# A hybrid decoder layer on one core: x transposed by the host, the surplus loop behind the last block, the last norm's sums on other engines

## The chip, the core and the metric

The kernel runs on one core of a Trainium2 chip. A core has TensorE (PE in the profile, its weight loads PEld), VectorE (DVE), ScalarE (ACT), GpSimd (POOL) and SyncE (SP), which here only issues transfers. Each engine works through its own list in order. The metric is the device time of one execution in microseconds; less is better. 0.2% of it is 2.7 us.

## The reference

One layer over 1024 positions of width 1024. The parts that this change touches are the head, the mixer's input, and the end:

```python
mod = silu(c) @ W_ada + b_ada            # shift/scale/gate of both sub-layers
h = x * (1 + scale1) + shift1
proj = h @ w_in                          # 3592 columns: DeltaNet q,k,v,z, beta, decay; attention q,k,v
mix = concat(gated_delta(proj), dilated_attention(proj)) @ w_o
x = layer_norm(ALPHA * x + (1 + gate1) * mix, ln1_g, ln1_b)
h = x * (1 + scale2) + shift2
y = sum over the top 2 of 8 experts of the best of 4 groups: gate * ((silu(h Wg) * (h Wu)) Wd)
x = layer_norm(ALPHA * x + (1 + gate2) * y, ln2_g, ln2_b)
```

## The kernel before

**Head.** x is kept with its 1024 features on the partitions, as eight column pieces (k) of 128 features in two halves (hf) of 512 positions. SP loads `x_` as eight row tiles of 512 KB, four of them ahead of the first 1024 columns x 2 of the modulation weights (`wad`, eight tiles of 1 MB, seven buffers) and four behind them. `x_cols` transposes each half on PE (L209) and copies it out of PSUM (L211, VectorE and ScalarE in turn). PE makes the shift and scale rows from `wad` (`pmod`), a transpose brings them to columns (`modc`, `s1`). Then, for each piece, ScalarE writes the rounded h (`hhi`, L247), VectorE the same in full precision (`ht`, L249), and their difference `hlo` (L251) is taken by VectorE for even k and by GpSimd for odd k.

**Projections.** 28 tasks of 128 columns each follow. A weight tile `wraw` is split into `whi` (ScalarE, L257) and `wlo` (GpSimd, L260), and 48 matmuls of 128x512 make one task: `hhi*whi`, `hlo*whi` and `hhi*wlo` for each piece. The weights of the first task are loaded between the seventh and the eighth `wad`. DeltaNet, attention, the output projection, the first norm and the router follow.

**Experts.** The slots are 81 blocks of 32 rows in the fixed order `SEQ`. A block's work is `block_gu` (64 matmul records `ph`), `block_h` (`pt`, `hT`), `block_d` (32 records `po`, scaled to `yo` on VectorE L1395) and a scatter of `yo` into `y2d` by GpSimd (L1346). In the loop the down projection of block n-1 stands between the up projection and the transpose of block n. Each expert's weights come as 4 MB (`wgu`, L1005) and 2 MB (`wd`, L1010) through SP into rings; after the last of them SP loads `xall`, the 4 MB of the residual (L1503), into a ring slot. Names such as `wgu<-x1d` or `wgu<-y2d` are such ring slots with other contents.

**Surplus loop.** Rows that found no place in the fixed blocks are handled in `overflow`, a loop whose trip count `nov` is read on the device. Every engine loads `novi` (L1398), compares and branches (L1450), and a barrier over all five engines that waits for the outstanding transfers stands at it. In the profiled execution its body is not run: the trace has 81 blocks. The call stands before the last block, after `down(n - 1)`.

**Last norm.** SP loads the norm's rows `lnb` (L1507), then the eight 1 MB pieces of `y2d` (L1531), one for each 128 positions t with the two expert outputs of a position, `ya` and `yb`. `combine(t)` adds them, on GpSimd for t in `PADD` (2, 5) and with PE and an identity into PSUM for the other six, adds the residual and sums (L1546, VectorE), and squares on ScalarE (L1549). `norm(t)` takes the inverse root on GpSimd (L465), applies the mean and the gain (L1556, VectorE) and the factor and offset: for t in `PSCALE` (1, 3, 5, 6) ScalarE L1558 and GpSimd L1559, for the others VectorE L1561. SP stores the result (L1562).

The order on each engine comes from the scheduler of the framework that builds the kernel; SP's and ACT's transfers share eight completion semaphores in turn, so a transfer waits for the one eight places ahead.

Of the kernel before, what the change touches and what calls it, by code (L numbers as in the profile page):

```python
# [20 lines left out]
P = 128  # L21
D = 1024
# [101 lines left out]
def build(nc, tc, I, out):  # L124
# [7 lines left out]
    with es:  # L132
# [25 lines left out]
        w_in = I["w_in"][0].rearrange("(k p) n -> p k n", p=P)  # L158
        wp = hps.enter_context(tc.tile_pool(name="wp", bufs=2, side="right"))

        def load_raw(col):
            raw = wp.tile([P, KD, P], F32, name="wraw", bufs=WR)
            SY.dma_start(raw, w_in[:, :, col:col + P])
            return raw
# [16 lines left out]
        xt = []  # L181

        def load_x(t):
            x_ = ap_.tile([P, D], F32, name="x_", bufs=NT)
            SY.dma_start(x_, I["x"][0, t * P:(t + 1) * P, :])
            xt.append(x_)
# [16 lines left out]
        hst, hlo = {}, {}  # L203

        def x_cols(hf, pool, tag):
            for k in range(KD):
                px = pool.tile([P, 4, P], F32, name=tag, bufs=3)
                for t in range(4):
                    T.transpose(px[:, t, :], xt[hf * 4 + t][:, k * P:(k + 1) * P], ident)  # L209
                hst[k, hf] = hp.tile([P, 512], F32, name="hlo", bufs=2 * KD + 1)  # L210
                (A.copy if k % 2 else V.tensor_copy)(hst[k, hf], px.rearrange("p a b -> p (a b)"))  # L211

        x_cols(0, pa, "px")
# [24 lines left out]
        V.tensor_scalar(s1, mcol[:, 8:16], 1.0, None, op0=OP.add)  # L238
        for hf in range(2):
            if hf == 1:  # L240
                pas.close()
                pps = ExitStack()
                pp = pps.enter_context(tc.tile_pool(name="pp", bufs=2, space=PSUM))
                x_cols(1, pp, "pg")
            for k in range(KD):
                sl_ = slice(hf * 512, hf * 512 + 512)
                A.activation(hhi[:, k, sl_], hst[k, hf], AF.Identity, bias=mcol[:, k:k + 1], scale=s1[:, k:k + 1])  # L247
# [138 lines left out]
        SY.dma_start(w8, w_in[:, :, 4 * GW:4 * GW + 8])  # L386
# [1103 lines left out]
        for n, (i, b_) in enumerate(blocks):  # L1490
# [17 lines left out]
            if n == nb - 1:  # L1508
                down(n - 1)
                overflow()  # L1510
# [16 lines left out]
        PSCALE = (1, 3, 5, 6)  # L1527
        PADD = (2, 5)
# [4 lines left out]
        def combine(t):  # L1533
            ya, yb = (yall[t // 4][:, t % 4, k] for k in range(2))
            if t in PADD:
                G.tensor_tensor(ya, ya, yb, op=OP.add)
                ps = ya
            else:
                ps = pf_.tile([P, D], F32, name="ps", bufs=4)
                for hf in range(2):  # L1540
                    for k, y_ in enumerate((ya, yb)):
                        mm(ps[:, 512 * hf:512 * hf + 512], ident, y_[:, 512 * hf:512 * hf + 512], start=(k == 0),
                           stop=(k == 1))
            xa = xall[:, t]
            mv = fp.tile([P, 8], F32, name="mv", bufs=4)
            V.tensor_tensor_reduce(xa, ps, xa, 1.0, 0.0, OP.add, OP.add, mv[:, 0:1])  # L1546
# [5 lines left out]
        def norm(t, mv):  # L1552
# [51 lines left out]
```

## Time and profile before

| | |
|---|---|
| time, median of 3 runs | 1374.77 us (1373.95 to 1376.49) |
| profiled execution | 1380.62 us, span 1378.8 us |
| busy in the span | PE 1206.5, PEld 823.5, DVE 622.7, POOL 435.3, ACT 334.0 us |
| mean granted TensorE clock | 0.941 |
| HBM read / written | 286.56 MB / 26.89 MB |

The span runs from the first to the last instruction; the profiled execution's own time has 1.8 us around it, and the median of the runs is 5.9 us below it. A row of the timeline gives start, busy time, engine, line, operation, output and inputs, count, and in brackets the idle time before it with what ended it. [...] Times in rows are microseconds from the start of the span.

### The profile page before, as it was taken

To read this page: it belongs to the slowest core of one execution; us is meant where nothing else is said; L and a number is where in the kernel's file an instruction comes from. 1 tells how busy PE (TensorE), PEld (TensorE's weight loads), DVE (VectorE), ACT (ScalarE), POOL (GpSimd) and SP (SyncE) were. 2 spreads that over 40 slices of the span, in tenths; PEclk is the share of its full clock that TensorE was granted. 3 is DMA by queue.
4 is the path that set the end of the run, shared out by engine and by line. 5 is a ranking of instruction groups with operands and counts; after the bars stand their busy time and mean duration, and the time that the engine had idled before them with its cause. 6 is when DMAs were issued, how large, how long until landed. Compare 5 with 4: busy or idle time off the path is not lost.

```text
span 1378.8 us, 32445 instructions
## 1 busy us (share of the span) xinstructions
PE 1206.5 (88%) x13949; PEld 823.5 (60%) x13949; DVE 622.7 (45%) x1414; ACT 334.0 (24%) x753; POOL 435.3 (32%) x410
## 2 busy tenths in 40 slices
PE   5889999999998989989889359898899999999662
PEld 2577787878785767867667235554455555555320
DVE  0867476583726747577986721111111111111126
ACT  1454343433322433344211101010011111111003
POOL 0613223322323404131542433332233333332116
PEclk8899999999999989999998679999999999999976
DMA  9311011110113435343336859999999999999763
GB/s 363 92 31 46 18 47 33 31 43 22 48 48 123 133 119 161 119 182 98 134 134 244 369 218 421 423 422 423 424 417 419 378 421 423 425 421 428 328 248 151
DMA packets 77189, 311.13 MB, mean 226 GB/s; under 512 B 11186, under 2 KB 47780, under 8 KB 67828
## 3 DMA queue, kind: packets, MB, share of 16 engines
q1 hardware_dynamic: 62624, 282.60, 52.3%
q0 software_dynamic: 8928, 21.00, 4.0%
q10 hardware_dynamic: 5492, 5.44, 1.2%
q8 instruction: 111, 1.82, 0.5%
q14 instruction: 34, 0.28, 0.1%
HBM read 286.56 MB, written 26.89 MB: 227 GB/s over the span
## 4 chain that ended last, share of the span: by engine, by line
PE 38%; DMA 13%; DVE 10%; issue 4%; POOL 4%; ACT 1%; POOLq 0%; ACTq 0%; SPq 0%; DVEq 0%
PE ph L128 16%; PE po L128 8%; DMA wd<-in_k_wd 8%; PE pj L128 5%; DMA araw<-in_w_ada 2%; DMA wgu<-x1d 2%; PE pc L128 2%; PE pg L128 2%; PE pt L1382 1%; DVE acc L276 1%; PE px L1362 1%; POOL wlo L260 1%; DVE oh L1037 1%; POOL mv L465 1%; PE pg L804 1%
## 5 line engine op out<-in xcount | busy, mean ns | idle before, releaser
L128 PE MATMUL ph<-wgu,xT 128*32 128x256 f32 x5184 | 300.1, 384 | 8.8 <-DMA wgu<-x1d 8.8
L128 PEld LDWEIGHTS ph<-wgu,xT 128*32 128x32 f32 x5184 | 160.7, 111 | 123.4 <-issue 26.8
L128 PE MATMUL pj<-hhi,whi 128*128 128x512 f32 x448 | 195.2, 436 | 4.4 <-ACT akq L517 2.4
L128 PE MATMUL pj<-hlo,whi 128*128 128x512 f32 x448 | 182.0, 406 | 3.4 <-DVE hlo L251 2.9
L128 PE MATMUL pj<-hhi,wlo 128*128 128x512 f32 x448 | 181.9, 406 | 0.0
L128 PE MATMUL po<-wd,hT 128*32 128x256 f32 x2592 | 157.5, 384 | 20.5 <-DMA wd<-in_k_wd 18.9
L260 POOL TENSOR_TENSOR wlo<-wraw,whi 128x256 fp32r<-128x256 f32 x112 | 95.7, 884 | 233.1 <-ACT whi L257 210.0
L1340 POOL DMA_INDIRECT xg<-h2d,idxt x81 | 82.6, 1020 | 273.4 <-PE px L1362 266.1
L1377 DVE TENSOR_TENSOR th<-th,ph 128x128 f32<-128x128 f32 x81 | 23.4, 288 | 312.7 <-ACT th L1376 312.7
L128 PEld LDWEIGHTS po<-wd,hT 128*32 128x32 f32 x2592 | 85.2, 111 | 78.3 <-issue 22.8
L1346 POOL DMA_INDIRECT y2d<-yo,sct x81 | 82.0, 1013 | 77.1 <-DVE hT L1384 36.0
L128 PEld LDWEIGHTS pj<-hhi,whi 128*128 128x128 f32 x448 | 86.2, 192 | 21.5 <-ACT akq L517 2.8
L128 PEld LDWEIGHTS pj<-hlo,whi 128*128 128x128 f32 x448 | 86.5, 193 | 19.6 <-DVE hlo L251 4.8
L128 PEld LDWEIGHTS pj<-hhi,wlo 128*128 128x128 f32 x448 | 85.8, 191 | 17.6 <-issue 0.5
L1395 DVE SCALAR_TENSOR_TENSOR yo<-po,gat,g2t 128x256 f32<-128x256 f32 x81 | 39.2, 484 | 116.7 <-PE po L128 116.7
L1376 ACT ACTIVATE th<-ph 128x128 f32<-128x128 f32 x81 | 22.5, 278 | 273.6 <-PE ph L128 273.6
L1364 ACT COPY xT<-px 128x256 f32<-128x256 f32 x81 | 30.2, 373 | 205.8 <-PE px L1362 205.8
L128 PE MATMUL pg<-akq 128*128 128x512 f32 (+3 forms) x96 | 40.6, 538 | 9.1 <-DVE sm L789 6.4
L128 PE MATMUL pj<-wohi,mhi 128*128 128x512 f32 x112 | 46.7, 417 | 0.0
L128 PE MATMUL pj<-wo,mhi 128*128 128x512 f32 x112 | 46.3, 413 | 0.0
L128 PE MATMUL pj<-wohi,mlo 128*128 128x512 f32 x112 | 45.3, 405 | 0.0
L128 PE MATMUL pc<-vtk,PT 128*128 128x128 f32 x288 | 39.5, 282 | 5.4 <-ACT PT L806 5.0
(718 smaller groups left out, 1838.2 us busy)
## 6 DMA issues: line engine op xcount, KB each, us to landing
wgu<-in_k_wgu SPq DMA_DIRECT2D x32, 4096.0 KB, 25.6
wd<-in_k_wd SPq DMA_DIRECT2D x32, 2048.0 KB
araw<-in_w_ada SPq DMA_DIRECT2D x32, 512.0 KB, 4.0
wraw<-in_w_in SPq DMA_DIRECT2D x28, 512.0 KB, 4.1
wad<-in_w_ada SPq DMA_DIRECT2D x8, 1024.0 KB, 9.6
wgu<-y2d SPq DMA_DIRECT2D x8, 1024.0 KB, 17.0
xr<-in_x SPq DMA_DIRECT2D x8, 512.0 KB
x1d<-xh POOLq DMA_DIRECT2D x8, 512.0 KB, 2.9
```

The lines of the kernel that those rows point to most:

```text
L128: return T.matmul(o, l, r, start=start, stop=stop)
L260: G.tensor_tensor(lo[:, k:k + 2], raw[:, k:k + 2], hi[:, k:k + 2].bitcast(F32), op=OP.subtract)
L276: V.scalar_tensor_tensor(state["acc"], raw, sc[:, k:k + 1], state["acc"], op0=OP.mult, op1=OP.add)
L465: G.tensor_tensor(o, x, e.to_broadcast(list(x.shape)), op=OP.pow)
L804: T.transpose(p[:, b_ - b0, :], sc_[:, b_ * P:(b_ + 1) * P], ident)
L1037: V.tensor_scalar(o_, e_, f_, None, op0=OP.is_equal)
L1340: G.indirect_dma_start(out=xg, out_offset=None, in_=h2v, in_offset=bass.IndirectOffsetOnAxis(ap=idx, axis=0), bounds_check=4 * S - 1, oob_ ...
L1346: G.indirect_dma_start(out=y2v[b_], out_offset=bass.IndirectOffsetOnAxis(ap=idx, axis=0), in_=yo, in_offset=None, bounds_check=8 * S - 1, ...
L1364: A.copy(xT, px)
L1376: A.activation(th, ph[:, 0], AF.Silu)
L1377: V.tensor_tensor(th, th, ph[:, 1], op=OP.mult)
L1395: V.scalar_tensor_tensor(yo, po, gcol, g2t, op0=OP.mult, op1=OP.mult)
```

## The change

The host hands over x already transposed (`k_xt`, partition = feature within a piece, then half, piece, position), the projection weights regrouped so that a task's tile is one run of 4 KB on each partition (`k_win`), and the eight small columns likewise (`k_w8`). The loads of x, `x_cols`, its 64 transposes and its 16 copies go. SP loads the first task's weights, then all eight `wad` (eight buffers), then x in four pieces of 1 MB. For odd k the full-precision h is now made by ScalarE, and all sixteen differences are taken by VectorE.

```diff
-        for t in range(4):
-            load_x(t)
+        first_w = load_raw(GW)
         wad = []
         for k in range(KD):
-            w = ap_.tile([P, 2048], F32, name="wad", bufs=KD - 1)
+            w = ap_.tile([P, 2048], F32, name="wad", bufs=KD)
             SY.dma_start(w, I["w_ada"][0, k * P:(k + 1) * P, 0:2048])
             wad.append(w)
-            if k == KD - 2:
-                first_w = load_raw(GW)
-        for t in range(4, NT):
-            load_x(t)
+        xT = ap_.tile([P, 2, KD, 512], F32, name="xT", bufs=1)
+        for hf in range(2):
+            for k in range(0, KD, 4):
+                SY.dma_start(xT[:, hf, k:k + 4], I["k_xt"][:, hf, k:k + 4])
...
-                ht = ap_.tile([P, 512], F32, name="ht", bufs=3)
-                V.tensor_scalar(ht, hst[k, hf], s1[:, k:k + 1], mcol[:, k:k + 1], op0=OP.mult, op1=OP.add)
-                hlo[k, hf] = hp.tile([P, 512], F32R, name="hlo", bufs=2 * KD + 1)
-                (G if k % 2 else V).tensor_tensor(hlo[k, hf], ht, hhi[:, k, sl_].bitcast(F32), op=OP.subtract)
+                x_ = xT[:, hf, k]
+                A.activation(hhi[:, k, sl_], x_, AF.Identity, bias=mcol[:, k:k + 1], scale=s1[:, k:k + 1])
+                ht = ap_.tile([P, 512], F32, name="ht", bufs=2)
+                if k % 2:
+                    A.activation(ht, x_, AF.Identity, bias=mcol[:, k:k + 1], scale=s1[:, k:k + 1])
+                else:
+                    V.tensor_scalar(ht, x_, s1[:, k:k + 1], mcol[:, k:k + 1], op0=OP.mult, op1=OP.add)
+                hlo[k, hf] = hp.tile([P, 512], F32R, name="hlo", bufs=2 * KD)
+                V.tensor_tensor(hlo[k, hf], ht, hhi[:, k, sl_].bitcast(F32), op=OP.subtract)
```

The surplus loop is called after the last block:

```diff
-            if n == nb - 1:
-                down(n - 1)
-                overflow()
             gx(n + XB - 1)
             th = block_gu(xp_, pm_, xTs.pop(n), wts[i][0])
...
-            if 0 < n < nb - 1:
+            if n:
                 down(n - 1)
...
         down(nb - 1)
+        overflow()
```

In the last norm VectorE adds the two expert outputs for t in `DADD`; PE adds them for the other six, and for t in `ASUM` also the residual, which ScalarE then copies out of PSUM while it sums. The factor and offset are VectorE's for all eight t.

```diff
-        PSCALE = (1, 3, 5, 6)
-        PADD = (2, 5)
+        DADD, ASUM = (0, 4), (1, 3, 5, 7)
...
-            if t in PADD:
-                G.tensor_tensor(ya, ya, yb, op=OP.add)
+            xa = xall[:, t]
+            if t in DADD:
+                V.tensor_tensor(ya, ya, yb, op=OP.add)
...
-                    for k, y_ in enumerate((ya, yb)):
+                    ys = (xa, ya, yb) if t in ASUM else (ya, yb)
+                    for k, y_ in enumerate(ys):
...
-            V.tensor_tensor_reduce(xa, ps, xa, 1.0, 0.0, OP.add, OP.add, mv[:, 0:1])
+            if t in ASUM:
+                A.activation(xa, ps, AF.Identity, accum_out=mv[:, 0:1])
+            else:
+                V.tensor_tensor_reduce(xa, ps, xa, 1.0, 0.0, OP.add, OP.add, mv[:, 0:1])
...
-            if t in PSCALE:
-                A.mul(xa, xa, mv[:, 4:5])
-                G.tensor_tensor(xa, xa, lnb[:, 1], op=OP.add)
-            else:
-                V.scalar_tensor_tensor(xa, xa, mv[:, 4:5], lnb[:, 1], op0=OP.mult, op1=OP.add)
+            V.scalar_tensor_tensor(xa, xa, mv[:, 4:5], lnb[:, 1], op0=OP.mult, op1=OP.add)
```

Three places show how the lists move; between them every engine's list is the same as before. First, SP's list at the program's start, before (`kc` holds the constants, `wraw` projection weights, `wad` modulation weights):

```order
L137 DMA kc<-in_k_main 128x896
L185 DMA x__90<-in_x 128x1024
L185 DMA x__92<-in_x 128x1024
L185 DMA x__94<-in_x 128x1024
L185 DMA x__96<-in_x 128x1024
L193 DMA wad<-in_w_ada 128x2048 x7
L163 DMA wraw<-in_w_in 128x8x128
L193 DMA wad<-in_w_ada 128x2048
L185 DMA x__116<-in_x 128x1024
```

and in the changed kernel:

```order
L137 DMA kc<-in_k_main 128x896
L162 DMA wraw<-in_k_win 128x1024
L184 DMA wad<-in_w_ada 128x2048 x8
L189 DMA xT<-in_k_xt 128x2048 x4
L369 DMA w_279<-in_k_w 128x64
L162 DMA wraw<-in_k_win 128x1024 x2
```

The four row tiles of x no longer stand ahead of `wad`, the projection weights moved from inside it to ahead of it, and x follows.

Second, PE's list at the surplus loop, before. The rows from the second branch to `REGISTER_ALU` are the loop's body and exit:

```order
L128 MATMUL ph<-wgu_13100,xT 32x256 x32
L128 MATMUL po<-wd_11591,hT 32x256 x16
L1382 MATMUL pt<-kc,th 128x128
L128 MATMUL po<-wd_13328,hT 32x256 x16
L1398 TENSOR_LOAD novi
L1450 COMPARE_AND_BRANCH
...
L1450 REGISTER_ALU
L1450 COMPARE_AND_BRANCH
L1450 UNCONDITIONAL_BRANCH
L128 MATMUL ph<-wgu_13255,xT 32x256 x32
L1382 MATMUL pt<-kc,th 128x128
L128 MATMUL po<-wd_13468,hT 32x256 x16
```

and in the changed kernel:

```order
L128 MATMUL ph<-wgu_12977,xT 32x256 x32
L128 MATMUL po<-wd_11468,hT 32x256 x16
L1365 MATMUL pt<-kc,th 128x128
L128 MATMUL ph<-wgu_13132,xT 32x256 x32
L128 MATMUL po<-wd_13205,hT 32x256 x16
L1365 MATMUL pt<-kc,th 128x128
L128 MATMUL po<-wd_13345,hT 32x256 x16
L1381 TENSOR_LOAD novi
L1433 COMPARE_AND_BRANCH
```

The last block's `ph`, `pt` and `po` moved from behind the loop to ahead of it, and its `ph` now follows the block before without a gap. GpSimd's last scatter still stands behind the loop.

Third, GpSimd's list behind the loop, before (`y2d<-yo` a scatter, L465 the inverse root, L1536 and L1559 the norm's adds):

```order
L1346 DMA y2d<-yo,sct 8192x256 x2
L1536 TENSOR_TENSOR wgu_13992<-wgu_13992 128x1024
L465 TENSOR_TENSOR mv<-mv,pio_64 128x1 x2
L1536 TENSOR_TENSOR wgu_13993<-wgu_13993 128x1024
L465 TENSOR_TENSOR mv<-mv,pio_64 128x1
L1559 TENSOR_TENSOR wgu_13470<-wgu_13470,wd_13668 128x1024
L465 TENSOR_TENSOR mv<-mv,pio_64 128x1
L1559 TENSOR_TENSOR wgu_13470<-wgu_13470,wd_13668 128x1024
```

and in the changed kernel:

```order
L1433 REGISTER_ALU
L1433 COMPARE_AND_BRANCH
L1433 UNCONDITIONAL_BRANCH
L1329 DMA y2d<-yo,sct 8192x256
L448 TENSOR_TENSOR mv<-mv,pio_64 128x1 x8
```

One scatter is left behind the loop instead of two, and of the norm GpSimd keeps only the eight inverse roots.

## Rows read from the trace of the kernel before

**Rows 1.** Busy time of each engine in two long stretches (start:end, length, then busy us and count for PE, PEld, DVE, ACT, POOL; granted clock, share of the transfer engines in use, GB/s).

```profile
100.00:400.00 300.00, 288.24 (x3762) 229.05 (x3761) 178.87 (x395) 109.27 (x244) 88.39 (x114) 1.00 0.13 35
1000.00:1290.00 290.00, 285.91 (x4878) 163.65 (x4870) 48.22 (x149) 32.01 (x99) 95.77 (x95) 1.00 0.99 415
```

**Rows 2.** The timeline of the head, in order of time.

```profile
6.08 0.90 PE L209 MATMUL px<-kc,x__90 128*128 128x128 f32 x3 [1.79 <-DMA x__90<-in_x]
...
11.50 0.90 PE L209 MATMUL px<-kc,x__96 128*128 128x128 f32 x3 [0.60 <-DMA x__96<-in_x]
...
26.75 1.93 PE L128 MATMUL pmod<-wad,sc 128*32 128x512 f32 x8 [0.54 <-DMA wad<-in_w_ada]
...
29.36 1.93 PE L128 MATMUL pmod<-wad,sc 128*32 128x512 f32 x8 [0.68 <-DMA wad<-in_w_ada]
...
33.56 1.93 PE L128 MATMUL pmod<-wad,sc 128*32 128x512 f32 x8 [2.26 <-DMA wad<-in_w_ada]
...
37.88 5.75 ACT L247 ACTIVATE hhi<-hlo,modc,s 128x512 fp32r<-128x512 f32 x8 [5.78 <-DVE s L238]
...
54.68 0.63 PE L128 MATMUL pj<-hhi,whi 128*128 128x512 f32 x1
55.10 0.63 PE L128 MATMUL pj<-hlo,whi 128*128 128x512 f32 x1
...
60.74 0.40 PE L128 MATMUL pj<-hhi,wlo 128*128 128x512 f32 x1
```

**Rows 3.** The instructions on `hlo` between 30 and 62 us: line, engine, operation, count, then duration in ns as least/median/most, first and last start, form.

```profile
L247 ACT ACTIVATE hhi<-hlo,modc,s x16: 798/802/816, 37.9 to 54.7; 128x512 fp32r<-128x512 f32 x16
L249 DVE TENSOR_SCALAR ht<-hlo,s,modc x16: 534/749/1511, 37.9 to 58.1; 128x512 f32<-128x512 f32 x16
...
L251 DVE TENSOR_TENSOR hlo<-ht,hhi x8: 679/680/1154, 38.8 to 58.5; 128x512 fp32r<-128x512 f32 x8
L251 POOL TENSOR_TENSOR hlo<-ht,hhi x8: 1454/1600/1609, 39.5 to 58.7; 128x512 fp32r<-128x512 f32 x8
```

**Rows 4.** The timeline around the surplus loop: the up projections of two blocks in turn on PE, the last scaling ahead of the loop on VectorE, and the first scatter behind the loop.

```profile
1289.39 3.66 PE L128 MATMUL ph<-wgu,xT 128*32 128x256 f32 x64
...
1295.19 3.66 PE L128 MATMUL ph<-wgu,xT 128*32 128x256 f32 x64
...
1303.39 0.48 DVE L1395 SCALAR_TENSOR_TENSOR yo<-po,gat,g2t 128x256 f32<-128x256 f32 x1 [2.06 <-PE po L128]
...
1312.70 0.98 POOL L1346 DMA_INDIRECT y2d<-yo,sct  x1 [10.31 <-issue]
```

**Rows 5.** Instructions of the surplus loop's two lines, engine by engine: duration in ns as least/median/most, first and last start. The first row is of line 1398, the second of line 1450.

```profile
L1398 DVEq TENSOR_LOAD <-novi x1: 540/540/540, 1303.6 to 1303.6; - x1
...
L1450 POOLq INC_SWDGE_SEM  x1: 1421/1421/1421, 1302.2 to 1302.2; - x1
```

**Rows 6.** The chain that ended last, from the load of the residual to the end: start, length, what.

```profile
1283.62 27.80 DMA wgu<-x1d
1311.42 0.70 issue
1312.12 6.20 PE ph L128 x64
...
1322.47 2.29 DMA y2d<-yo,sct
1324.83 4.87 DMA wgu<-y2d
...
1329.83 5.88 PE ps L128 x8
...
1372.73 1.28 DVE wgu L1561
```

**Rows 7.** Transfers between 1200 and 1379 us by what they move: queue, count, size each where known, median us from issue to landing.

```profile
wd<-in_ln_g SPq DMA_DIRECT2D x1, 512.0 KB, 3.9
...
y2d<-yo,sct POOLq DMA_INDIRECT x20, 10.4
```

**Rows 8.** The last norm's groups between 1325 and 1379 us: line, engine, operation, form, count, busy us, mean ns, idle time before and what ended it.

```profile
L128 PE MATMUL ps<-wgu,kc 128*128 128x512 f32 x48 | 23.0, 644 | 8.2 <-DMA wgu<-y2d 8.2
...
L465 POOL TENSOR_TENSOR mv<-mv,pio 128x1 f32<-128x1 f32 x8 | 9.2, 1153 | 8.8 <-DVE mv L1554 8.8
L1549 ACT ACTIVATE sq<-wgu,mv 128x1024 f32<-128x1024 f32 x8 | 9.2, 1144 | 32.4 <-DVE mv L1547 23.4 <-DVE mv L1554 9.0
L1546 DVE CUSTOM_DVE_ANT_0 wgu<-ps,wgu 128x1024 f32<-128x1024 f32 x6 | 7.3, 1218 | 13.6 <-PE ps L128 13.6
L1561 DVE SCALAR_TENSOR_TENSOR wgu<-wgu,mv,wd 128x1024 f32<-128x1024 f32 x4 | 7.2, 1803 | 3.6 <-POOL mv L465 3.6
...
L1549 ACT ACTIVATION_READ_ACCUMULATOR sq<-wgu,mv 128x1 f32 x8 | 1.5, 186 | 0.0
L1554 DVE TENSOR_SCALAR mv<-mv 128x1 f32<-128x1 f32 x8 | 1.2, 147 | 6.3 <-ACT sq L1549 6.3
```

**Rows 9.** The timeline of the last norm: two of PE's weight loads soon after its start, and GpSimd's first add, of t = 2.

```profile
1331.67 0.34 PEld L128 LDWEIGHTS ps<-wgu,kc 128*128 128x128 f32 x1 [0.52 <-issue]
...
1332.53 0.34 PEld L128 LDWEIGHTS ps<-wgu,kc 128*128 128x128 f32 x1 [0.52 <-issue]
...
1334.89 2.35 POOL L1536 TENSOR_TENSOR wgu<-wgu 128x1024 f32<-128x1024 f32 x1 [11.44 <-DMA wgu<-y2d]
```

More of the change, by code (lines that the diff above doesn't have):

```diff
@@ L156, in build @@
         rc = p1.enter_context(tc.tile_pool(name="rc", bufs=1))
-        w_in = I["w_in"][0].rearrange("(k p) n -> p k n", p=P)
         wp = hps.enter_context(tc.tile_pool(name="wp", bufs=2, side="right"))
@@ L162, in load_raw @@
             raw = wp.tile([P, KD, P], F32, name="wraw", bufs=WR)
-            SY.dma_start(raw, w_in[:, :, col:col + P])
+            SY.dma_start(raw, I["k_win"][WCOLS.index(col)].rearrange("p (k n) -> p k n", n=P))
             return raw
@@ L202, in build @@
                         I["b_ada"][0:1, j * 512:(j + 1) * 512].to_broadcast([32, 512]))
[L203 to L213, printed above, removed]
+        hlo = {}
         pc8 = pa.tile([P, KD], F32, name="pc8", bufs=1)
@@ L238, in build @@
         V.tensor_scalar(s1, mcol[:, 8:16], 1.0, None, op0=OP.add)
+        pas.close()
+        pps = ExitStack()
+        pp = pps.enter_context(tc.tile_pool(name="pp", bufs=2, space=PSUM))
         for hf in range(2):
[L240 to L244, printed above, removed]
             for k in range(KD):
                 sl_ = slice(hf * 512, hf * 512 + 512)
-                A.activation(hhi[:, k, sl_], hst[k, hf], AF.Identity, bias=mcol[:, k:k + 1], scale=s1[:, k:k + 1])
-                ht = ap_.tile([P, 512], F32, name="ht", bufs=3)
-                V.tensor_scalar(ht, hst[k, hf], s1[:, k:k + 1], mcol[:, k:k + 1], op0=OP.mult, op1=OP.add)
-                hlo[k, hf] = hp.tile([P, 512], F32R, name="hlo", bufs=2 * KD + 1)
-                (G if k % 2 else V).tensor_tensor(hlo[k, hf], ht, hhi[:, k, sl_].bitcast(F32), op=OP.subtract)
+                x_ = xT[:, hf, k]
[7 more added lines that the diff above has]
+                V.tensor_tensor(hlo[k, hf], ht, hhi[:, k, sl_].bitcast(F32), op=OP.subtract)
         a0.close()
@@ L385, in build @@
         w8 = rc.tile([P, KD, 8], F32, name="w8")
-        SY.dma_start(w8, w_in[:, :, 4 * GW:4 * GW + 8])
+        SY.dma_start(w8, I["k_w8"])
         wc = gp.tile([P, KD, 16], F32R, name="W", bufs=2)
@@ L1571, in build @@
         mes.close()
-_INS = ["x", "c", "positions", "w_ada", "b_ada", "w_in", "conv_w", "a_log", "dt_bias", "gdn_norm_w",
+_INS = ["x", "c", "positions", "w_ada", "b_ada", "conv_w", "a_log", "dt_bias", "gdn_norm_w",
         "attn_norm_w", "w_o", "ln1_g", "ln1_b", "w_router_group", "b_router_group", "w_router_expert",
@@ L1584, in expert_arrays, with proj_arrays @@
     return {"k_wgu": np.ascontiguousarray(gu), "k_wd": np.ascontiguousarray(d)}
+QB = 4 * GW + 8
+WCOLS = [128 * j for j in range(16)] + [QB + 128 * j for j in range(12)]
+def proj_arrays(x, w_in):
+    xt = np.asarray(x)[0].reshape(2, 512, KD, P).transpose(3, 0, 2, 1)
+    w = np.asarray(w_in)[0].reshape(KD, P, -1)
+    win = np.stack([w[:, :, c:c + P] for c in WCOLS]).transpose(0, 2, 1, 3).reshape(len(WCOLS), P, KD * P)
+    w8 = w[:, :, 4 * GW:4 * GW + 8].transpose(1, 0, 2)
+    return {"k_xt": np.ascontiguousarray(xt), "k_win": np.ascontiguousarray(win), "k_w8": np.ascontiguousarray(w8)}
 def kernel(**inputs):
@@ L1594 @@
     data.update(const_arrays())
+    data.update(proj_arrays(inputs["x"], inputs["w_in"]))
     data.update(expert_arrays(inputs["w_gate"], inputs["w_up"], inputs["w_down"]))
```

8 lines of the change are left out of this document (1 added, 7 removed).

## The prediction

> **What bounds the kernel now.** I read the stage table first. Between 100 and 400 us PE is busy 288 of 300 us at a granted clock of 1.00; between 1000 and 1290 us the transfer engines are in use 0.99 of the time [rows 1]. The reader is to see two long stretches with a bound of their own, and the lists of all engines between the head and the last blocks are unchanged. So the middle neither gains nor loses. It begins when the head lets it, since its loads wait for buffers that the stage before frees; what the head saves moves all the rest forward. The sum is therefore head plus tail. The head's timeline [rows 2] shows PE waiting for each modulation tile, and the chain of waits [rows 6] shows the tail as one line: residual load, last block, scatter, read of `y2d`, last norm.
>
> **Head: the modulation weights.** The first x tile is used at 6.08 and the fourth at 11.50 [rows 2]. Now the first projection tile, as large as one x tile, stands in the first one's place and the other three are gone: 11.50 - 6.08 = 5.4 us at most, since the small transfers of ScalarE's queue that shared this time remain. The last `wad` followed the seventh by 33.56 - 29.36 = 4.2 us, the seventh the sixth by 29.36 - 26.75 = 2.61 us; the half megabyte between them, and the wait for a seventh buffer, cost 1.6 us and go. That makes 7.0 us at the top. By bytes alone, 2 MB fewer at 2.61 us each, it is 5.2 us. I take 6.3: the last `wad` at 27.3. From its use to the first `hhi` the chain took 37.88 - 33.56 = 4.3 us and is unchanged, so `hhi` starts at 31.6.
>
> x must be there. Its four pieces land 2.61 us apart behind `wad`: 29.9, 32.5, 35.1, 37.7. They are needed at 31.6 and then about every 4.3 us. The margin is smallest for the first, 1.7 us, and it moves with `wad`, so I charge nothing; if the first piece came 3 us later than this, 1.3 us would show.
>
> **Head: h and the first task.** ScalarE now makes 24 tiles, eight of which took 5.75 us before [rows 2], 0.72 each although one lasts 0.80 [rows 3]: 17.3 us, ending at 48.9. VectorE makes 8 `ht` at 0.53, the least value, now that no GpSimd subtraction runs beside it, and 16 differences at 0.68 [rows 3]: 15.1 us, covered by ScalarE. GpSimd's 1.6 us per odd piece is gone. The last difference and three matmuls add 1.6 us: the task ends at 50.5, against 60.74 + 0.40 = 61.1 before, 10.6 us earlier. PE itself needs 48 matmuls; at 1.2 GHz they follow each other in 0.43 us (54.68 to 55.10 [rows 2]), 20.6 us in all, so if PE stays at that level it ends near 32.3 + 20.6 = 52.9 and the gain is 8.2. A slow start costs part of that; I take **10.2 us**, bounds 6.9 (5.2 for the weights, half clock) and 11.3 (7.0 for the weights). The second task's weights are now split after the 24 tiles, at 49 instead of 43; the 32 small matmuls on `w8` stand ahead of that task on PE and cover it. The 64 transposes and 16 copies filled PE and VectorE only while weights were awaited or the first task was starved, so I give them no gain of their own. The 4 KB rows of `k_win` I also cost at nothing: each task's weights come two tasks ahead.
>
> **Tail: the surplus loop.** Before, the last `yo` ahead of the loop ends at 1303.87 [rows 4] and PE resumes at 1312.12. The chain says why: the residual's load, issued at 1283.62, lands at 1311.42, and 0.70 us later PE goes on [rows 6]. The loop's own work is short: 0.54 us to load the count on VectorE, 1.42 us for GpSimd's semaphores [rows 5]. In the changed kernel one more block runs in that wait: `ph` 3.66, then `po` and `yo`; from one block's `ph` to the next is 1295.19 - 1289.39 = 5.8 us [rows 4], so `yo` ends at 1309.7 (all times on the old axis, the head's gain aside). With 0.54 us for the count that is still before 1311.42. The last scatter, which stood at 1322.47, then starts where the first one behind the loop does, 1312.70 [rows 4, 6]: 9.8 us earlier.
>
> It now shares the transfer engines with the two norm rows, issued just ahead and landing in 3.9 us [rows 7]. Alone the scatter took 2.29 us to land [rows 6]; beside the full weight stream the median was 10.4 [rows 7]. I take 3.3, nearer the first, since 1 MB is ahead and not a stream: reads of `y2d` issued at 1316.0 instead of 1324.83, **8.8 us** earlier, bounds 1.7 (the median of 10.4) and 9.8. [...] No row here shows a scatter beside so short a load.
>
> **Tail: the last norm.** The first piece lands 4.87 us after the issue [rows 6], at 1320.9; the third landed at 1334.89 [rows 9], so they come 2.6 us apart. PE has 4 x 6 + 2 x 4 = 32 calls instead of 24. Its 48 records before were 24 calls; the first eight took 5.88 us (1.47 a call) and the other forty 23.0 - 5.88 = 17.2 us, 0.86 a call [rows 6, 8]. One call on the residual runs early; five on t = 1 take 5.88 + 0.86 from 1323.5 and end at 1330.2; 26 more at 0.86 end at 1352.6. Behind the last: ScalarE's copy and square (1.34 each, the 1.14 of a square and 0.19 to read its sum), three small steps of 0.15, two products of 1.28 [rows 6, 8]: 1358.4.
>
> VectorE has 2 adds and 4 sums with the residual at 1.22, 16 products at 1.28 and 20 small steps of 0.15 or less: 30.5 us. In its list order with the waits for ScalarE's sums and PE, t = 0 is done at 1327.9, t = 1 waits for PE until 1331.5, and from there it is seldom idle; each t brings its ready times late by part of a product. Walking the list with these durations I get the last product's end at 1361.2. Before, it ended at 1372.73 + 1.28 = 1374.0. Of the 12.8 us between them 8.8 are the loop's and **4.0 us** the norm's. What pays is GpSimd: the mean of four products beside its adds was 1.80 instead of 1.28, and its one-column roots lasted 1.15 us in the mean [rows 8]. The norm's term is bounded by PE alone (1358.4, so 6.8) and by nothing gained (0): the stalls go, but VectorE takes over four products and two adds. Scattered stores follow as before: 4.8 us behind the last product.
>
> **Sum.** 10.2 + 8.8 + 4.0 = 23.0 us. The profiled execution, 1380.6 (span 1378.8), becomes 1357.6. The median of the runs shown is 5.9 lower than it, so the time is 1374.8 - 23.0 = **1352 us**. By its own bounds the forecast spans 8.6 to 27.9 us of gain, 1366.2 to 1346.9.
>
> **Rivals.**
> *The loop has a price of its own.* If the 8.2 us from 1303.87 to 1312.12 were loop entry and exit, PE would resume 5.8 us later than I say: 1357.6. For it: the drain of all queues stands there. Against: the chain's last step is the residual's landing, and the loop's own instructions last one or two microseconds [rows 5, 6]. Chance 0.10.
> *The head keeps half its gain.* If the stretch from 62 us on is set by a chain that started before the first task ended, or x is late, only 5 us arrive: 1357. Chance 0.12.
> *The adds run at 1.2 GHz.* PE is idle for more than 10 us before them. The early weight loads of the norm are 0.86 us apart, two to a call [rows 9], so 1.7 us a call: 5 + 26 calls from 1323.5 end at 1376.2, the last product near 1382.0, 8.0 us later than before. With the other 10.2 saved: 1372.6, no measurable change. [...] Against: in the trace before the level rose during the first eight records and stayed [rows 6, 8], and the calls for one t (3.4 or 5.2 us) outlast the 2.6 us between landings. Chance 0.03.
> *The expert stream gets slower.* The new arrays stand ahead of the expert weights in memory. The stream moves 201 MB at 415 GB/s [rows 1], 485 us; a loss of 1% costs 4.9 us, from 5% on it outweighs the gain, and 6% gives 1352 + 29 = 1381. For it: that stretch has no slack. Against: the weights keep their order and rows. Chance 0.03, and the only way to slower.
> The forecast has the remaining 0.72.
>
> **How the numbers follow.** The range of 1345 to 1362 holds most of the forecast and both smaller gains. 0.2%, 2.7 us, is about what a measurement can tell from no change. Faster: 0.72 + 0.10 + 0.12 = 0.94. Within: 0.03. Slower: 0.03.
>
> **What would show it.** Right: the last `pmod` group near 27, the first `hhi` near 31.6, the last matmul of the first task near 50.5; the stage from 100 us on as before, about 10 us earlier; the residual's landing still last ahead of the loop, and the scatter within 1.5 us of it; the norm from the first read to the last product 45 us instead of 49, with VectorE's products all near 1.28. Wrong: an `hhi` waiting for x, a gap behind the loop that no transfer explains, adds 1.7 us a call throughout, or a read of the stage after 62 us that starts less than 8 us earlier.

## The result and the profile after

The changed kernel takes 1356.38 us in the median of four runs (1352.82 to 1359.02), against 1374.97 for the kernel before beside it: a ratio of 0.9862, 95% interval 0.9837 to 0.9887, or 19 us less. The forecast was 1352, its range 1345 to 1362. The profiled execution took 1359.02 us, span 1357.2.

The two long stretches first, moved by ten microseconds, in the columns of [rows 1].

```profile
90.00:390.00 300.00, 287.25 (x3753) 227.92 (x3753) 179.22 (x395) 108.11 (x243) 87.86 (x114) 1.00 0.11 35
990.00:1280.00 290.00, 286.80 (x4879) 163.80 (x4871) 47.82 (x148) 32.14 (x99) 95.59 (x94) 0.99 0.99 415
```

At this grain nothing changed: the expert weights still come at 415 GB/s. It is too coarse, as will be seen, for the first stretch.

The timeline of the head (start, busy time, engine, line, operation, count, idle time before and what ended it) answers to [rows 2]: the last modulation tile, the first `hhi`, the last matmul of the first task.

```profile
28.25 1.79 PE L128 MATMUL pmod<-wad,sc 128*32 128x512 f32 x8 [0.55 <-DMA wad<-in_w_ada]
...
31.98 1.52 ACT L227 ACTIVATE hhi<-xT,modc,s 128x512 fp32r<-128x512 f32 x2 [20.68 <-DVE s L219]
...
50.17 0.40 PE L128 MATMUL pj<-hhi,wlo 128*128 128x512 f32 x1
```

The first task ends at 50.57, 10.6 us earlier. The tiles that make h (least/median/most in ns, first and last start) answer to [rows 3]:

```profile
L234 DVE TENSOR_TENSOR hlo<-ht,hhi x16: 691/692/694, 32.8 to 49.1; 128x512 fp32r<-128x512 f32 x16
L232 DVE TENSOR_SCALAR ht<-xT,s,modc x8: 545/545/549, 32.0 to 46.3; 128x512 f32<-128x512 f32 x8
L230 ACT ACTIVATE ht<-xT,modc,s x8: 801/806/810, 33.4 to 48.2; 128x512 f32<-128x512 f32 x8
```

Every duration now has one value; the 749 ns median of `ht` and the GpSimd row are gone.

Around the loop, SP's own issues, and then the end of the chain that ended last (answering to [rows 6]):

```profile
1274.86 0.43 SPq L1486 DMA_DIRECT2D wgu<-x1d  x1
1303.02 0.35 SPq L1490 DMA_DIRECT2D wd<-in_ln_g  x1
...
1309.34 6.67 SPq L1511 DMA_DIRECT2D wgu<-y2d  x8
```

```profile
1294.18 4.36 issue
1298.78 3.18 DMA y2d<-yo,sct
1303.54 5.78 DMA y2d<-yo,sct
1309.76 6.99 DMA wgu<-y2d
1316.79 6.15 PE ps L128 x10
```

SP leaves the loop 28.2 us behind the residual's issue, as before (1311.85 - 1283.62 = 28.2). Two transfers now land nearly together ahead of it: the residual at 1301.68 and, 0.3 us later, the scatter of 1298.78, which is the one that the chain names. The scatter behind the loop starts half a microsecond later and takes 5.78 us to land, against 2.29. The groups of the last norm (count, busy us, mean ns, idle time before) answer to [rows 8]:

```profile
L128 PE MATMUL ps<-wgu,kc 128*128 128x512 f32 x62 | 28.5, 622 | 8.8 <-DMA wgu<-y2d 8.8
...
L448 POOL TENSOR_TENSOR mv<-mv,pio 128x1 f32<-128x1 f32 x8 | 11.9, 1485 | 34.7 <-DVE mv L1538 34.7
L1540 DVE SCALAR_TENSOR_TENSOR wgu<-wgu,mv,wd 128x1024 f32<-128x1024 f32 x8 | 10.2, 1281 | 0.0
L1541 DVE SCALAR_TENSOR_TENSOR wgu<-wgu,mv,wd 128x1024 f32<-128x1024 f32 x8 | 10.2, 1281 | 1.3 <-POOL mv L448 1.3
```

VectorE's sixteen products last 1.28 us each. From the first read of `y2d` to the last product's end it is 43.1 us (1309.34 to 1352.42), before 49.2.

### The profile page after: what moved, and what is told of

It reads as the page before. It is cut to its first block, busy times and chain, and to the rows that moved or that the text cites. A ratio compares the mean times of both kernels' runs of the same rounds, so it can differ in the third digit from the quotient of the medians.

```text
span 1357.2 us, 32321 instructions
## 1 busy us (share of the span) xinstructions
PE 1201.2 (89%) x13901; PEld 813.3 (60%) x13901; DVE 616.0 (45%) x1404; ACT 335.1 (25%) x757; POOL 409.3 (30%) x396
## 3 DMA queue, kind: packets, MB, share of 16 engines
q8 instruction: 111, 1.82, 0.5%
## 4 chain that ended last, share of the span: by engine, by line
PE 40%; DMA 11%; DVE 10%; issue 4%; POOL 3%; ACT 1%; POOLq 0%; SPq 0%; ACTq 0%; DVEq 0%
PE ph L128 17%; PE po L128 9%; DMA wd<-in_k_wd 8%; PE pj L128 5%; DMA araw<-in_w_ada 2%; PE pc L128 2%; PE pg L128 2%; PE pt L1365 1%; DVE acc L259 1%; PE px L1345 1%; POOL wlo L243 1%; DVE oh L1020 1%; DMA y2d<-yo,sct 1%; PE pg L787 1%; ACT sq L1533 1%
## 5 line engine op out<-in xcount | busy, mean ns | idle before, releaser
L1323 POOL DMA_INDIRECT xg<-h2d,idxt x81 | 82.6, 1020 | 273.2 <-PE px L1345 265.9
L128 PEld LDWEIGHTS pj<-hhi,whi 128*128 128x128 f32 x448 | 85.5, 191 | 23.1 <-ACT akq L500 2.8
L128 PEld LDWEIGHTS pj<-hhi,wlo 128*128 128x128 f32 x448 | 85.4, 191 | 17.2 <-issue 0.9
L128 PE MATMUL pg<-akq 128*128 128x512 f32 (+3 forms) x96 | 40.7, 539 | 10.2 <-DVE sm L772 6.1
## 6 DMA issues: line engine op xcount, KB each, us to landing
wad<-in_w_ada SPq DMA_DIRECT2D x8, 1024.0 KB, 10.3
```

The costliest lines, as they stand in the source:

```text
L128: return T.matmul(o, l, r, start=start, stop=stop)
L1323: G.indirect_dma_start(out=xg, out_offset=None, in_=h2v, in_offset=bass.IndirectOffsetOnAxis(ap=idx, axis=0), bounds_check=4 * S - 1, oob_ ...
```

## The experiments

Each kernel was profiled once, and timed in five rounds beside the kernel before. They ran in three groups, each with its own runs of the kernel before: head, loop, norm and rows late; no loop, three sums, offset on GpSimd and PE kept at work; the last four. Only the last group has the changed kernel itself in it, so in the other two a time is set beside the changed kernel's through the ratios alone. The stage from the residual's load to the end is compared by this table, worked out from the timelines of SP, GpSimd and VectorE, in us: the residual's issue; from it to the first read of `y2d`; from the last scatter's start to that read; from the read to the last product's end; from the residual's issue to the end of the span.

| kernel | residual issued | to read | scatter to read | read to product | residual to end |
|---|---|---|---|---|---|
| before | 1283.62 | 41.2 | 2.4 | 49.2 | 95.2 |
| head alone | 1270.68 | 39.7 | 2.4 | 48.9 | 93.4 |
| loop alone | 1277.48 | 34.4 | 5.3 | 48.4 | 87.6 |
| norm alone | 1278.88 | 41.2 | 2.4 | 44.2 | 90.3 |
| changed | 1274.86 | 34.5 | 5.8 | 43.1 | 82.3 |
| changed again | 1269.92 | 34.7 | 6.2 | 44.5 | 84.0 |
| rows late | 1273.09 | 32.1 | 3.6 | 45.0 | 82.0 |
| no loop | 1274.49 | 31.4 | 5.3 | 44.4 | 80.6 |
| three sums | 1276.90 | 33.4 | 4.9 | 42.0 | 80.2 |
| offset on GpSimd | 1276.54 | 34.4 | 6.1 | 48.7 | 87.9 |
| PE kept at work | 1276.32 | 34.2 | 5.8 | 41.4 | 80.5 |
| joined | 1276.95 | 32.6 | 4.1 | 41.6 | 79.0 |
| half of x first | 1278.89 | 33.9 | 5.0 | 43.8 | 82.6 |
| differences on GpSimd | 1280.80 | 34.3 | 5.1 | 43.7 | 82.9 |

The first column is a finding in itself: lists that agree up to the residual's load issue it anywhere between 1269.9 and 1277.0 with the new head (the last two rows have heads of their own), and between 1277.5 and 1283.6 with the old. One pair of profiles does not give the head's gain at that place.

**Head alone.** The changed kernel with the loop and the norm put back. Of the edit only the loop's call is shown; the norm's lines are those of the change, reversed.

```diff
+            if n == nb - 1:
+                down(n - 1)
+                overflow()
...
-        overflow()
```

> The changed kernel with the surplus loop and the last norm put back as before, so the head alone. Theory (the three parts add up, the middle only moves forward): 8.8 us less than before, the shift that the residual's load shows in the changed kernel (1283.62 to 1274.86), 7.5 to 10 allowed; first task ends near 50.6, residual's load near 1274.9, loop exit and norm as before from there. Rival (part of the head's 10.6 us is given back later whatever stands behind): 5 us less. Rival (the parts do not add): less than 3 or more than 12.

Ratio 0.9947 (0.9931 to 0.9963), 7.3 us less (5.1 to 9.5). Between the theory's 8.8 and the first rival's 5, just under the 7.5 that the theory allowed; the interval rules out neither 8.8 nor a little over 5.

**Loop alone.** The kernel before with the call moved.

```diff
-            if n == nb - 1:
-                down(n - 1)
-                overflow()
...
         down(nb - 1)
+        overflow()
```

> The kernel before with only the surplus loop moved behind the last block. Theory: 6.7 us less; the loop is left when the residual lands (near 1311.4 as before), the one scatter behind it takes 5 to 6 us to land beside the two norm rows, reads of y2d near 1318. Rival (the loop has a price of its own): 3 us less, and PE or SP go on 5 us or more behind the residual's landing. Rival (the scatter as first forecast, 3.3 us): 8.8 us less.

Ratio 0.9945 (0.9927 to 0.9963), 7.6 us less (5.1 to 10.0). By the time alone the theory's 6.7 and the second rival's 8.8 can't be told apart; the scatter tells them apart. Its chain, from the scatter behind the loop:

```profile
1306.57 5.32 DMA y2d<-yo,sct
1311.91 4.82 DMA wgu<-y2d
```

The scatter behind the loop is as slow without the other two parts: 5.3 us, as the theory had it.

**Norm alone.** The kernel before with the new `combine` and `norm`; only the sets of t are shown here, the other lines are those of the change.

```diff
-        PSCALE = (1, 3, 5, 6)
-        PADD = (2, 5)
+        DADD, ASUM = (0, 4), (1, 3, 5, 7)
```

> The kernel before with only the last norm's new division of work. Theory: 6.1 us less, 43.1 us instead of 49.2 from the first read of y2d to the last product. Rival (VectorE takes over what GpSimd gives up and becomes the bound): 0 to 4 us less; the forecast's own figure was 4.0.

Ratio 0.9960 (0.9943 to 0.9976), 5.5 us less (3.3 to 7.8), 44.2 us from read to product instead of 49.2. That lies nearer the theory's 6.1, though the interval reaches down to the rival's 4. The three parts alone sum to 20.4 us, the whole gave 19.0 (15.5 to 22.4), and 17.2 (15.1 to 19.3) when run again: they add, as far as this can tell.

**Rows late.** The norm's rows behind the first two reads.

```diff
-                    SY.dma_start(lnb[:, j], I[n_].to_broadcast([P, D]))
...
             SY.dma_start(yall[t // 4][:, t % 4], y2r[t])
+            if t < 2:
+                SY.dma_start(lnb[:, t], I["ln2_" + "gb"[t]].to_broadcast([P, D]))
```

> The changed kernel with the two loads of the norm's rows issued behind the first and the second read of y2d instead of ahead of the last scatter. Theory (the scatter lands late because these 1 MB share the transfer engines with it): the scatter lands in 2.3 to 2.9 us instead of 5.8, the reads start 3 to 3.5 us earlier, 3 us less than the changed kernel, 1.5 if the pieces behind the rows come too late for VectorE. Rival (the scatter is slow behind the loop for a reason of its own): landing stays near 5.8 us, no change within 0.7 us.

```profile
1301.55 3.62 DMA y2d<-yo,sct
1306.12 8.50 DMA wgu<-y2d
```

With nothing of SP's ahead the scatter lands in 3.62 us: 2.2 of its 3.5 us of delay came from the rows. The theory had 2.3 to 2.9 us; the other 1.3 us stay open. The read comes 2.4 us sooner, but the second piece, now behind a row, lands 8.50 us after its issue instead of 6.99, and it is the one PE waits for. 82.0 us to the end instead of 82.3, median 1356.10, ratio 0.9851 (0.9829 to 0.9874): no gain that the runs can tell. The wait moved by one transfer.

**No loop.**

```diff
         down(nb - 1)
-        overflow()
```

> The changed kernel without the surplus loop (leaves out rows that would find no place in the fixed blocks). The tail runs from the residual's load to the end of the span: 82.3 us in the changed kernel. Theory (the loop only waits for the last landing): with no exit to wait for, the last scatter starts at the last yo, 2 to 3 us sooner, and lands beside the end of the residual and the two rows; tail 79 to 81.5. Rival (the loop has a price of its own): tail 76 or less. Rival (nothing, since the transfers bound this place): 82 to 83.

SP's issues:

```profile
1274.49 0.43 SPq L1486 DMA_DIRECT2D wgu<-x1d  x1
...
1305.92 6.85 SPq L1510 DMA_DIRECT2D wgu<-y2d  x8
```

The read comes 3.1 us sooner and the stage ends 1.7 us sooner (80.6), where the theory put it; ratio 0.9823 (0.9800 to 0.9846). A price of eight microseconds for the loop itself is refuted; what it still costs is these 1.7 us.

**Three sums.**

```diff
-        DADD, ASUM = (0, 4), (1, 3, 5, 7)
+        DADD, ASUM = (0, 4), (1, 3, 5)
```

> The changed kernel with the residual of t = 7 added and summed by VectorE again, so two PE calls of 0.86 us fewer. Theory (PE sets the end of the last norm: its last sums end at 1345.2, 7.2 us ahead of the last product): PE ends 1.7 us sooner and so does the span, tail 80.6 instead of 82.3. Rival, as the forecast had it (VectorE is the longer list): no gain or up to 1.2 us more, tail 82.3 to 83.5.

PE's list ends 34.6 us behind the first read instead of 35.9, and the last product 42.0 instead of 43.1, though VectorE has one sum more. That is the theory's direction and two thirds of its size. It does not yet show PE as the bound: between its first step on the sum of t = 1 and the last product, VectorE is busy 24.2 of 26.8 us here and 23.1 of 28.3 in the changed kernel, so its waits fell by 2.6 us. Whether they fell because PE has less to do or because VectorE's list now has the sum of t = 7 to fill them with is not shown. The timed runs, 1359.49 and ratio 0.9865 (0.9833 to 0.9896), do not resolve it.

**Offset on GpSimd.**

```diff
-            V.scalar_tensor_tensor(xa, xa, mv[:, 4:5], lnb[:, 1], op0=OP.mult, op1=OP.add)
+            if t in (1, 3, 5, 6):
+                A.mul(xa, xa, mv[:, 4:5])
+                G.tensor_tensor(xa, xa, lnb[:, 1], op=OP.add)
+            else:
+                V.scalar_tensor_tensor(xa, xa, mv[:, 4:5], lnb[:, 1], op0=OP.mult, op1=OP.add)
```

> The changed kernel with factor and offset of t = 1, 3, 5, 6 on ScalarE and GpSimd again, as before. Theory (what pays is GpSimd out of VectorE's way): products beside GpSimd's adds last 1.8 us in the mean, the norm takes 3 to 5 us longer, tail 85 to 87. Rival (PE sets the end, GpSimd's adds lie beside it): the end moves by less than 1.5 us.

Its groups, in the columns of the norm's groups above:

```profile
L1540 DVE SCALAR_TENSOR_TENSOR wgu<-wgu,mv,wd 128x1024 f32<-128x1024 f32 x8 | 11.8, 1478 | 0.0
L1543 POOL TENSOR_TENSOR wgu<-wgu,wd 128x1024 f32<-128x1024 f32 x4 | 9.9, 2471 | 3.8 <-ACT wgu L1542 3.8
...
L1545 DVE SCALAR_TENSOR_TENSOR wgu<-wgu,mv,wd 128x1024 f32<-128x1024 f32 x4 | 7.3, 1814 | 1.4 <-POOL mv L448 1.4
```

48.7 us from read to product, the whole gain of the norm given back (the three profiles with the old norm have 48.4 to 49.2); ratio 0.9895 (0.9870 to 0.9921). Four products beside the adds last 1.81 us again. But slower products are not all of it: from its first step on the sum of t = 1 to the last product VectorE is busy 22.2 us, 0.9 less than in the changed kernel, and waits 10.3 instead of 5.2. PE's last sums, those of t = 7, end at 1348.32, and ScalarE takes them only at 1353.92, since the factor of t = 6 stands ahead of them in its list. The 87.9 us to the end are 0.9 more than the theory allowed.

**PE kept at work.** Eight products into the tile that t = 1's sums then overwrite.

```diff
                 ps = pf_.tile([P, D], F32, name="ps", bufs=4)
+                for _ in range(8 if t == 1 else 0):
+                    mm(ps[:, 0:512], ident, xa[:, 0:512], start=True, stop=True)
```

> The changed kernel with eight more products of the residual by the identity (their result is overwritten) ahead of t = 1's sums, so that PE works while the first pieces of y2d are on their way. Theory (the first three weight loads of t = 1 stand 0.86 us apart, at half clock, all later ones 0.43): all of t = 1's at 0.43, its sums 1.8 us sooner, PE's list and the span 1.3 to 1.8 us sooner, tail 80.5 to 81. Rival (VectorE sets the end): tail within 0.5 of 82.3. Rival (the eight end after the piece has landed): t = 1 later, tail 83 or more.

The last step of its chain:

```profile
1317.88 4.57 PE ps L128 x10
```

Ten records take 4.57 us instead of 6.15 (7.51 in the changed kernel's second profile), and the last product ends 41.4 us behind the read instead of 43.1 (44.5): beside the first profile 1.6 us at PE, 1.7 at the end. The granted clock is 1.00 over these ten records; in the changed kernel it is 0.50 over the first 3.0 us of them. So a slow start of t = 1 on PE is paid in full at the end. That does not make PE the bound of what follows, since VectorE's list hangs on the same sum: from VectorE's first step on it to the last product it is 28.3 us in this kernel and in the changed one alike. The median of 1357.35, ratio 0.9852 (0.9826 to 0.9878), does not show so little.

**Half of x first.**

```diff
+        for k in range(0, KD, 4):
+            SY.dma_start(xT[:, 0, k:k + 4], I["k_xt"][:, 0, k:k + 4])
         wad = []
...
-        for hf in range(2):
-            for k in range(0, KD, 4):
-                SY.dma_start(xT[:, hf, k:k + 4], I["k_xt"][:, hf, k:k + 4])
+        for k in range(0, KD, 4):
+            SY.dma_start(xT[:, 1, k:k + 4], I["k_xt"][:, 1, k:k + 4])
```

> The changed kernel with the first half of x (2 MB, transposed by the host) loaded ahead of the modulation weights instead of behind them. Theory (megabytes ahead of the weights cost 2.6 us each): the last modulation weight and the first hhi 5.2 us later (37.2 instead of 32.0), the first task ends at 55.8 instead of 50.6, whole time 3.5 to 5 us more than the changed kernel. Rival (the gain of the head comes from the transposes and copies that went, not from the order of the loads): first task within 1 us of 50.6, no change of the time.

The first `hhi`, and the first task's last matmul:

```profile
36.98 1.52 ACT L228 ACTIVATE hhi<-xT,modc,s 128x512 fp32r<-128x512 f32 x2 [26.02 <-DVE s L220]
...
55.18 0.40 PE L128 MATMUL pj<-hhi,wlo 128*128 128x512 f32 x1
```

Both 5.0 us later: the order of the loads is worth 5.0 of the head's 10.6. The time is 1360.21 beside 1357.10 for the changed kernel in the same rounds, ratio 0.9891 (0.9876 to 0.9906): 3.1 us of the 5.0 in the medians, just under the 3.5 that the theory allowed.

**Differences on GpSimd.**

```diff
-                V.tensor_tensor(hlo[k, hf], ht, hhi[:, k, sl_].bitcast(F32), op=OP.subtract)
+                (G if k % 2 else V).tensor_tensor(hlo[k, hf], ht, hhi[:, k, sl_].bitcast(F32), op=OP.subtract)
```

> The changed kernel with GpSimd taking the difference of the odd pieces again, as before. Theory (ScalarE's 24 tiles set the pace of the first task, GpSimd's 1.6 us per odd piece lie beside them): first task ends within 1 us of 50.6. Rival (GpSimd in VectorE's way was what held the first task): VectorE's ht near 0.75 us instead of 0.55, first task ends 2 us later or more. The scheduler also swaps a few neighbours in the middle, so the reading is the first task's end.

```profile
L232 DVE TENSOR_SCALAR ht<-xT,s,modc x8: 545/546/548, 32.1 to 47.6; 128x512 f32<-128x512 f32 x8
L234 DVE TENSOR_TENSOR hlo<-ht,hhi x8: 693/1228/1239, 32.9 to 48.6; 128x512 fp32r<-128x512 f32 x8
...
L234 POOL TENSOR_TENSOR hlo<-ht,hhi x8: 1273/1341/1349, 34.4 to 50.2; 128x512 fp32r<-128x512 f32 x8
```

The first task ends at 52.27, 1.7 us later, between the two forecasts and by neither one's account: `ht` stays at 0.545, it is VectorE's own difference that goes from 0.69 to 1.23 beside GpSimd's, and PE's last wait in the task, 0.56 us, is for a difference of GpSimd's. The forecast's reason for a short `ht`, that no GpSimd subtraction runs beside it, is not borne out here. The time, 1357.76, is that of the changed kernel.

**Joined, and the changed kernel again.** Six products that keep PE at work, three sums, and both rows behind the second read; only the rows' lines are shown.

```diff
+            if t == 1:
+                for j, n_ in enumerate(("ln2_g", "ln2_b")):
+                    SY.dma_start(lnb[:, j], I[n_].to_broadcast([P, D]))
```

> The changed kernel with six products of the residual ahead of t = 1 that keep PE at work, three sums on ScalarE instead of four, and the two norm rows loaded behind the second read of y2d. Theory (PE sets the end of the norm, the rows ahead slow the scatter): scatter lands in 3.6 us, t = 1 starts 2 us sooner and wholly at the higher clock, PE ends 4 to 5 us sooner, tail from the residual's load to the end 77 to 78.5 instead of 82.3, 4 to 5 us less than the changed kernel. Rival (VectorE becomes the bound as soon as PE is faster): tail 79.5 to 80.5. Rival (pieces behind the rows come too late for PE): tail 81 or more.

> The changed kernel, unchanged, beside the three others on the same chip: ratio 0.986 to the kernel before; every theory expects the same, its spread says what a difference of two runs is worth.

The joined kernel takes 1351.84 us, the changed one beside it 1357.10: ratios to the kernel before of 0.9835 (0.9822 to 0.9849) and 0.9875 (0.9860 to 0.9890), intervals that do not meet, 5.3 us between the medians. PE's rows of the joined kernel's norm:

```profile
1308.08 7.96 PE L128 MATMUL ps<-wgu,kc 128*128 128x512 f32 x14 [5.48 <-issue]
1316.89 4.56 PE L128 MATMUL ps<-wgu,kc 128*128 128x512 f32 x10 [0.85 <-DMA wgu<-y2d]
1323.02 20.87 PE L128 MATMUL ps<-wgu,kc 128*128 128x512 f32 x48 [1.57 <-DMA wgu<-y2d]
```

Between two of its forecasts (79.0 us to the end): t = 1 runs at a granted clock of 1.00 throughout, but the third piece, behind the rows, is now 1.57 us late. It is faster than both kernels; which of its three edits gives how much was not timed apart.

## Why the prediction was nearly right

**The top of the head: right, at the low end of its bounds.** The last `wad` is used at 28.25 (forecast 27.3), 5.3 us earlier; that is the bound "by bytes alone" of 5.2, and half of x put back ahead costs 5.0. x is never waited for. The first task ends at 50.57 (forecast 50.5): from the first `hhi` it is 18.6 us, and ScalarE's last of 24 tiles ends at 49.0 (forecast 48.9). Of the 10.6 us the order of the loads is 5.0, and GpSimd's differences 1.7 when put back; what the transposes and copies that went and ScalarE's half of `ht` are worth was not tested apart. A slip of no consequence: the lower bound of 6.9 should read 7.1 by its own terms (8.2, less 1.1 for the weights).

**"So the middle neither gains nor loses": this step failed.** The mean over the three profiles with the old head and the nine with the new, at instructions that both have, on ScalarE or SP (within a column the profiles spread by 6 to 7 us at the residual's load):

| place, us before | old head | new head | gain |
|---|---|---|---|
| load of the positions, 60 | 60.6 | 49.8 | 10.8 |
| copy of `W`, 156 | 155.8 | 147.4 | 8.4 |
| `sq`, 349 | 346.8 | 340.8 | 6.0 |
| residual's load, 1284 | 1280.0 | 1274.4 | 5.6 |

In the 300 us behind the first task PE waits 13.2 us in the mean with the old head and 15.8 with the new; of that, waits that name no releaser ("issue") are 0.2 and 2.5. They stand at the same few places of PE's list, most of them inside groups of 64 small matmuls, one near 300 us at a matmul of 128x512. PE in the kernel with the head alone:

```profile
136.09 0.43 PE L128 MATMUL pg<-Xc,BL 32*32 32x32 f32 x27
137.29 0.52 PE L128 MATMUL pg<-Xc,BL 32*32 32x32 f32 x37 [0.76 <-issue]
...
140.46 0.38 PE L128 MATMUL pg<-Xc,BL 32*32 32x32 f32 x20
141.25 0.59 PE L128 MATMUL pg<-Xc,BL 32*32 32x32 f32 x44 [0.41 <-issue]
```

and the first of these groups in the kernel with the loop alone, whose head is the old one:

```profile
147.01 0.75 PE L128 MATMUL pg<-Xc,BL 32*32 32x32 f32 x64
```

The new head's cuts lie behind the 27th and the 20th matmul in the changed kernel too. From one to the next are 128 matmuls, each with its weight load: 256 instructions. The page of the changed kernel counts the instruction transfers:

```profile
q8 instruction: 111, 1.82, 0.5%
```

1.82 MB in 111 transfers is 16 KB each. The same page counts 13901 matmuls and 13901 weight loads; if all 111 transfers carry PE's list, that is, as an estimate, 250 instructions to a transfer, and the distance of the cuts agrees. The author's reading is that the list comes in pieces of this size: the change took instructions out of it ahead of this place, so it would be cut elsewhere, here within bursts that last 0.75 us. The times of the transfers fit too. The fourteen profiles have 55 such waits of PE of over 0.12 us between 100 and 1270 us, all of them before 305 us, lasting 0.14 to 2.17 us. Every one of them ends 1.2 to 1.6 us behind the end of the last instruction transfer, while the transfers themselves lie 3 to 32 us apart there. That the load of the next instructions ends these waits is inferred from distance, the estimate of size and this constant lag; no row names it, and no run moved the cuts on purpose. Some 2.3 of the 4.8 us lost by 349 are these waits. The rest of the loss is open; the regrouped weights are not seen in it, since none of PE's waits in these 300 us is for a transfer. The timed head, 7.3 us (5.1 to 9.5), stands between the forecast's 10.2 and its second rival, "the head keeps half its gain", which had 5 us and the time of 1357: nearer in size than the forecast, though by another mechanism than the chain it named; the interval leaves out 10.2 and, barely, 5.

**The loop: the mechanism right, one size wrong.** The loop is left when the last transfer has landed, with or without the last block in front; it was the residual before, and is now the residual with a scatter 0.3 us behind it. SP goes on 0.4 us after that landing before, and 1.1 us now; the scatter behind the loop starts 1.6 us after it, just over the 1.5 that the forecast gave as a sign of being right. What failed is "I take 3.3" for the scatter's landing beside the two rows: 4.9 to 6.2 us in the profiles of the new order, 3.6 and 4.1 where the rows were moved behind. The term was 6.8 us at the read (41.2 to 34.4) instead of 8.8, inside its bounds.

"No row here shows a scatter beside so short a load" holds for the rows shown, not for the trace they were read from. In the kernel before, the first scatter behind the loop, that of 1312.70 [rows 4], was issued 0.85 us behind the first of the two rows. The transfers issued between 1311 and 1314 us there, in the columns of [rows 7]:

```profile
wd<-in_ln_g SPq DMA_DIRECT2D x1, 512.0 KB, 3.9
wd<-in_ln_b SPq DMA_DIRECT2D x1, 512.0 KB
y2d<-yo,sct POOLq DMA_INDIRECT x1, 6.0
```

With 6.0 in place of 3.3 the term is 9.8 + 2.3 - 6.0 = 6.1 us. The norm alone, which keeps the old order, has 5.97 at the same place.

**The norm: the walk of VectorE's list was right to a microsecond, its price of GpSimd is not shown.** Seven profiles have the new norm as it is (changed, changed again, norm alone, rows late, no loop, half of x first, differences on GpSimd): 43.1 to 45.0 us from the read to the last product, 44.1 in the mean, against 48.8 in the mean of the three with the old norm (48.4 to 49.2). That is 4.7 us, and 5.5 timed, where the forecast had 4.0. VectorE's first step on the sum of t = 1 comes 14.8 us behind the read in the changed kernel and 15.4 to 16.8 in the six others (forecast 15.5). From there to the last product it is 28.3 us in all seven (forecast 29.7: the walk charged 1.4 us too much). The changed kernel from VectorE's second small step for t = 1 to its first for t = 6, in the columns of [rows 1]:

```profile
1325.58:1343.52 17.94, 17.94 (x43) 7.94 (x42) 17.60 (x27) 7.20 (x12) 7.37 (x5) 1.00 0.69 277
```

VectorE is busy 17.6 of 17.9 us, "seldom idle" as forecast. PE is busy throughout too, but none of VectorE's waits there is for PE. Behind this stretch VectorE waits 3.6 us in all for the squares and roots of the last two t. PE decides where this stretch starts: its first ten records behind the read last 6.15 us in the changed kernel, 7.51 in its second profile and 4.57 when it is kept at work, and the last product ends 29.5 us behind them in all three.

What the forecast gave as the reason, "what pays is GpSimd", is shown only in part. Factor and offset of four t put back on ScalarE and GpSimd give the whole gain back. But there VectorE has less to do and waits more, for ScalarE above all, so GpSimd in VectorE's way and ScalarE's fuller list are not told apart. GpSimd's eight roots, counted among the costs at 1.15 us, last longer in the changed kernel, 1.49 us.

**The sum.** 10.2 + 8.8 + 4.0 = 23.0 against 7.3 + 7.6 + 5.5 = 20.4 timed: two terms too large, one too small. Only the head's term lies outside its interval. That the errors have opposite signs and partly cancel is luck. The other rivals: the loop's price falls with the run without it. The adds at the lower clock were real for the first weight loads of t = 1 alone (granted clock 0.50 over 3.0 us), 1.6 us in one profile of the changed kernel and 2.9 in the other (6.15 and 7.51 against 4.57), not 1.7 us a call throughout. What the forecast calls 1.2 GHz is a granted clock of 0.50; no view gives a clock in GHz. In the kernel before, 128x512 matmuls follow each other in 0.43 us at 0.50 (54.68 to 57.24) and in 0.23 us at 1.00 (58.14 to 58.60). The expert stream kept its 415 GB/s.

## What to carry to other kernels

A gain at the head of a long chain has to be read again at its far end, over several profiles: here 10.8 us were 5.6 in the mean at the tail (7.3 timed), and two profiles of the same lists differ by up to 7 us there. Two loads of 512 KB issued just ahead of a small transfer that everything waits for cost it here 2.2 us of the 3.5 by which it landed later (3.62 us to landing without them, 5.78 with them); the trace of the kernel before may show the same pair in another place, as it did here. Moved behind the first two reads they made the second piece land in 8.50 us instead of 6.99, and it was the one that PE waited for. When a shorter list on one engine moves the end of a short tail, that engine need not be the bound: see first whether another engine's list starts from the same result, and whether that one waits at all behind it.

## What the hardware showed unexpectedly

PE waits of 0.2 to 0.8 us inside groups of short matmuls (64 in 0.75 us), two of them 256 instructions apart, and single ones of up to 2.2 us near 300 us, all ending 1.2 to 1.6 us behind an instruction transfer; that the same lists gained such waits from a shorter head was not foreseen. VectorE's subtraction of two 128x512 tiles takes 0.69 us in the changed kernel, which has none on GpSimd, and 1.23 us in the median beside GpSimd's, which takes 1.34, while its `ht`, with one tile and two columns as inputs, stays at 0.545 there; in the kernel before, also beside GpSimd's, the subtraction had a median of 0.68 and `ht` one of 0.75 [rows 3].
